# A float32 product in three parts becomes two: one of 512 columns, one of 256, and an add behind them

## Chip, cores and metric

The kernel runs on one NeuronCore of a Trainium2 chip, as one program. The time is device microseconds of one execution. The profile is one further execution under the hardware profiler, with its own time.

## The reference, cut to what matters

One sequence of 256 tokens (plus 16 meta tokens, 272 columns in all), width 1024, goes through two blocks in float32:

```python
h = h + mixer(rmsnorm(h))            # block 1: two kinds of attention, gates, w_up_a, w_up_b, w_o
h = h + hier_moe(rmsnorm(h))         #          router, then 32 experts of width 512
x = rmsnorm(h)[:, 16:]               # 256 tokens
h = h + retention_mixer(rmsnorm(h))  # block 2: 272 columns again, with its own meta tokens
h = h + swiglu(rmsnorm(h))           #          272 columns, hidden width 2816
h = h + mla_mixer(...)               #          keys over 272 columns, queries over 256
h = h + swiglu(rmsnorm(h))           #          256 columns
out = rmsnorm_2(h)[:, 16:]
```

Each `@` with a weight matrix is a dense projection; those are the subject here.

## The kernel before

Activations lie transposed: 128 features on the partitions, tokens along the free axis. `NM` = 16, `NX` = 256, `T` = 272. A dense projection works in tiles of 128 output features by `n` tokens, `n` being `T` or `NX`; each sums over `nkb` blocks of 128 input features (8 in most, 4 for `w_up_a`/`w_up_b` and the latent keys, 6 for the latent queries, 16 in the retention output, 22 in the feed-forward's second half).

Float32 is computed from two parts of the type float32r. A weight `w` is split as it arrives: ScalarE copies it to `wh` (L285), VectorE takes the rest, `wl = w - wh` (L286). The input is split in the same way into `xh`, `xl` (L285/L286, or L289/L290 with a gain). `tiles` then runs three products per weight block into one PSUM tile: `wh` by `xh` (L298), `wl` by `xh` (L299), `wh` by `xl` (L300), each of `n` columns and each with its own weight load (PEld in the profile). The tile is up to 272 columns of a PSUM bank of 512 float32; three such tiles are named `acc`, five `att`.

`dense` runs one output tile and, half way through, lets waiting generators take one step (`step`): attention, norms and transposes are written as generators that put their instructions between the projections. `begin` starts a stage with four tiles at once, first over `cut` blocks and then over the rest, so that it can start before the whole input is there; `dense` later hands those four out from `ready`. `project` adds an output to the residual `h` in two rounds, `cut` blocks first (L331), the others after the attention has ended (L336). What reads a finished tile is one VectorE or ScalarE instruction straight from PSUM: a multiply by the norm's row (L741 for the gates `sg`, L1208 and L1211 in the feed-forward, L1363 in the latent layer), `rope`'s copy (L423), the gated sums L755 and L756 in the loop over `pa` and `pb`, the residual L781 after `w_o`.

Weights come as a stream (`Stream`): fetched by DMA on SyncE's queue, split into one of five buffers of four blocks in the first block (`wsp1`), of three buffers of eight blocks in the second (`wsp2`). The expert weights (`raw<-in_wm`, 192 transfers of 1 MB) have 16 buffers, part of which lie in memory that the first block frees only when it ends.

The order of instructions on each engine is not the program's: the tile framework orders them by priority and by its own estimates of their durations when the kernel is built, and then sets the semaphores. On the chip each engine works through its list in that order.

Stages in time, by the profile: first block to about 229 us (projections, stick and sparse attention to 174, `pa`/`pb` to 198, `w_o` to 222, then the router), experts to about 710, retention, feed-forward over 272 columns, latent attention from about 1150 to 1296, feed-forward over 256 columns to 1484, final norm.

Of the kernel before, what the change touches and what calls it, by code (L numbers as in the profile page):

```python
# [16 lines left out]
P = 128  # L17
NM = 16
# [240 lines left out]
class Kern:  # L259
# [42 lines left out]
    def dense(self, ws, nkb, xh, xl, c0=0, n=T):  # L302

        if self.ready:
            return self.ready.pop(0)
        p = self.acc()
        self.tiles(ws, p, range(nkb // 2), nkb, xh, xl, c0, n)
        self.step()
        self.tiles(ws, p, range(nkb // 2, nkb), nkb, xh, xl, c0, n)
        return p[:, :n]  # L310

    def begin(self, ws, nkb, cut, xh, xl, cols, then=None, at=()):
# [3 lines left out]
        for i in range(8):  # L316
            p, (c0, n) = ps[i % 4], cols[i % 4]
            self.tiles(ws, p, range(cut) if i < 4 else range(cut, nkb), nkb, xh, xl, c0, n)
            if i in at:
                next(then, None)  # L320
        self.ready = [p[:, :n] for p, (_, n) in zip(ps, cols)]

    def project(self, ws, nkb, cut, xh, xl, c0, done):

        h, n = self.h, T - c0
        for b in range(KB):
            p = self.acc()
            self.tiles(ws, p, range(cut // 2), cut, xh, xl, 0, n)
            self.step()
            self.tiles(ws, p, range(cut // 2, cut), cut, xh, xl, 0, n)  # L330
            self.nc.vector.tensor_add(h[:, b, c0:], h[:, b, c0:], p[:, :n])  # L331
        self.flush()
        for b in range(KB):
            p = self.acc()
            self.tiles(ws, p, range(cut, nkb), nkb, xh, xl, 0, n, cut)
            self.nc.vector.tensor_add(h[:, b, c0:], h[:, b, c0:], p[:, :n])  # L336
# [125 lines left out]
    def mixer(self):  # L462
# [5 lines left out]
        with ctx:  # L468
# [21 lines left out]
            qb = m.tile([P, 4, NX], F32, name="qb")  # L490
# [38 lines left out]
            self.begin(ws, KB, 4, uh, ul, [(0, T)] * 3 + [(NM, NX)], self.rms(r, s, T, D, 1e-6), (4, 7))  # L529
# [6 lines left out]
            self.rope(kw, self.dense(ws, KB, uh, ul), T, perm, cr, sr)  # L536
            gps.memset(ckv[:, T:], 0.0)
            dve.tensor_mul(ckv[:, :T], self.dense(ws, KB, uh, ul), r)
            self.rope(ki, self.dense(ws, KB, uh, ul), T, perm, cr, sr)
# [32 lines left out]
            for b in range(4):  # L572
                self.rope(qi[:, b], self.dense(ws, KB, uh, ul, NM, NX), NX, perm, crx, srx)
# [33 lines left out]
            for b in range(4):  # L607
                if b < RAW:
                    self.expert_fetch()
                dve.tensor_mul(ka[b][:, :T], self.dense(ws, KB, uh, ul), r)  # L610
# [3 lines left out]
            for b in range(4):  # L614
                dve.tensor_mul(vt[:, b, :T], self.dense(ws, KB, uh, ul), r)
# [10 lines left out]
            for b in range(4):  # L626
                p = self.dense(ws, KB, uh, ul, NM, NX)
# [104 lines left out]
            self.gens.append(stick())  # L732
            for b in range(4):
                self.rope(qb[:, b], self.dense(ws, KB, uh, ul, NM, NX), NX, perm, crx, srx)
# [5 lines left out]
            for b in range(16):  # L740
                dve.tensor_mul(sg[b], self.dense(ws, KB, uh, ul, NM, NX), rx)  # L741
# [8 lines left out]
            for b in range(8):  # L750
                pa = self.dense(ws, 4, yah, yal, 0, NX)
                pb = self.dense(ws, 4, ybh, ybl, 0, NX)
# [25 lines left out]
            self.begin(ws, KB, 7, zh, zl, [(0, NX)] * 4)  # L778
            for b in range(8):
                p = self.dense(ws, KB, zh, zl, 0, NX)  # L780
# [12 lines left out]
            self.tiles(ws, pr, range(4), KB, hgh, hgl, 0, NX)  # L793
            rt = self.norm_end(self.colsum([s], NX), NX, D, 1e-6)
            self.tiles(ws, pr, range(4, KB), KB, hgh, hgl, 0, NX)
            lt = wk.tile([P, NX], F32, name="rp_raw")[:36]
            act(lt, pr[:36, :NX], AF.Copy)
# [396 lines left out]
    def ffn(self, u, s, c0, parts, c1, out=None):  # L1194
# [3 lines left out]
        uh, ul = u[:, 0], u[:, 1]  # L1198
# [307 lines left out]
```

## Time and profile before

| what | value |
| --- | --- |
| three runs | 1498.06, 1502.76, 1506.22 us; median 1502.76 |
| the profiled execution | 1498.93 us, span 1497.1 us |
| busy: TensorE, its weight loads, VectorE, ScalarE, GpSimd | 88%, 70%, 48%, 35%, 9% |
| granted TensorE clock, mean over the span | 0.931 of 2.4 GHz |
| DMA: moved, mean rate | 359.55 MB, 240 GB/s |

Busy shares are of the whole span. PE is TensorE's products, PEld its weight loads, which overlap them, DVE is VectorE, ACT ScalarE, POOL GpSimd, SP SyncE. A product's duration runs from its start to the modelled end of its result, so consecutive products overlap; how fast they go is read from the distance of their starts.

### The profile page before, as it was taken

To read this page: it belongs to the slowest core of one execution; us is meant where nothing else is said; L and a number is where in the kernel's file an instruction comes from. 1 tells how busy PE (TensorE), PEld (TensorE's weight loads), DVE (VectorE), ACT (ScalarE), POOL (GpSimd) and SP (SyncE) were. 2 spreads that over 40 slices of the span, in tenths; PEclk is the share of its full clock that TensorE was granted. 3 is DMA by queue.
4 is the path that set the end of the run, shared out by engine and by line. 5 is a ranking of instruction groups with operands and counts; after the bars stand their busy time and mean duration, and the time that the engine had idled before them with its cause. 6 is when DMAs were issued, how large, how long until landed. Compare 5 with 4: busy or idle time off the path is not lost.

```text
span 1497.1 us, 23804 instructions
## 1 busy us (share of the span) xinstructions
PE 1314.9 (88%) x9734; PEld 1051.7 (70%) x9734; DVE 724.4 (48%) x1417; ACT 528.3 (35%) x903; POOL 134.3 (9%) x165
## 2 busy tenths in 40 slices
PE   7999998776776666666999999999999999999997
PEld 7898993220221212104999999999999999899997
DVE  7866673110100101004666665766666865766654
ACT  5476651000000000004333443544444544544442
POOL 4010020000000000002121111100000211100001
PEclk9999998895787878778999999999999999999998
DMA  8443668999999999997434344454455433355551
GB/s 309 128 130 111 225 241 361 420 419 373 420 420 421 421 420 421 421 420 319 142 116 146 134 141 145 151 183 169 169 174 185 164 113 135 123 192 171 193 186 73
DMA packets 55266, 359.55 MB, mean 240 GB/s; under 512 B 6384, under 2 KB 7024, under 8 KB 15600
## 3 DMA queue, kind: packets, MB, share of 16 engines
q1 hardware_dynamic: 55152, 357.97, 63.2%
q8 instruction: 78, 1.28, 0.3%
q14 instruction: 36, 0.29, 0.1%
HBM read 356.90 MB, written 1.05 MB: 239 GB/s over the span
## 4 chain that ended last, share of the span: by engine, by line
PE 47%; DVE 2%; ACT 1%; issue 0%; POOL 0%; DVEq 0%; ACTq 0%; POOLq 0%
PE acc L298 14%; PE acc L300 14%; PE acc L299 14%; DVE wl L286 1%; ACT wh L285 1%; PE att L414 0%; PE att L1487 0%; PE att L1304 0%; PE att L1280 0%; PE att L383 0%; DVE U L290 0%; PE att L1306 0%; PE att L1397 0%; PE att L1294 0%; PE att L1305 0%
## 5 line engine op out<-in xcount | busy, mean ns | idle before, releaser
L298 PE MATMUL acc<-U,wh 128*128 128x272 f32 (+1 forms) x1456 | 424.0, 291 | 12.3 <-ACT U L289 7.2
L299 PE MATMUL acc<-U,wl 128*128 128x272 f32 (+1 forms) x1456 | 417.7, 287 | 2.5 <-DVE wl L286 2.5
L300 PE MATMUL acc<-U,wh 128*128 128x272 f32 (+1 forms) x1456 | 417.9, 287 | 0.0
L286 DVE TENSOR_TENSOR wl<-raw,wh 128x1024 fp32r<-128x1024 f32 x232 | 285.2, 1230 | 154.7 <-ACT wh L285 154.2
L285 ACT ACTIVATE wh<-raw 128x1024 fp32r<-128x1024 f32 x232 | 245.6, 1060 | 314.3 <-PE acc L300 211.2
L298 PEld LDWEIGHTS acc<-U,wh 128*128 128x128 f32 x1456 | 276.6, 190 | 17.6 <-ACT U L289 7.4
L299 PEld LDWEIGHTS acc<-U,wl 128*128 128x128 f32 x1456 | 275.9, 189 | 3.1 <-DVE wl L286 3.0
L300 PEld LDWEIGHTS acc<-U,wh 128*128 128x128 f32 x1456 | 275.9, 190 | 0.4
L983 PE MATMUL acc<-raw,U 128*32 128x512 f32 x1024 | 186.2, 820 | 91.0 <-DMA raw<-in_wm 87.3
L983 PEld LDWEIGHTS acc<-raw,U 128*32 128x32 f32 x1024 | 24.5, 124 | 238.1 <-DMA raw<-in_wm 214.7
L994 DVE TENSOR_TENSOR hid<-hid,acc 128x512 f32<-128x512 f32 x8 | 5.5, 688 | 258.1 <-PE acc L983 258.1
L300 PE MATMUL acc<-hl,wh 128*128 128x272 f32 (+1 forms) x352 | 99.5, 283 | 0.0
L299 PE MATMUL acc<-hh,wl 128*128 128x272 f32 (+1 forms) x352 | 99.3, 282 | 0.0
L298 PE MATMUL acc<-hh,wh 128*128 128x272 f32 (+1 forms) x352 | 99.1, 281 | 0.0
L1009 PE MATMUL att<-raw,ht 128*32 128x512 f32 x512 | 68.6, 635 | 28.7 <-DMA raw<-in_wm 25.1
L286 DVE TENSOR_TENSOR wl<-rawh,wh 128x512 fp32r<-128x512 f32 x112 | 80.5, 734 | 25.3 <-ACT wh L285 25.2
L285 ACT ACTIVATE wh<-rawh 128x512 fp32r<-128x512 f32 x112 | 68.2, 627 | 41.0 <-PE acc L300 24.9
L1018 DVE TENSOR_TENSOR h<-h,att 128x512 f32<-128x512 f32 x32 | 22.0, 688 | 123.9 <-PE att L1016 123.9
L298 PEld LDWEIGHTS acc<-hh,wh 128*128 128x128 f32 x352 | 66.4, 188 | 0.0
L300 PEld LDWEIGHTS acc<-hl,wh 128*128 128x128 f32 x352 | 66.1, 188 | 0.0
L299 PEld LDWEIGHTS acc<-hh,wl 128*128 128x128 f32 x352 | 66.1, 188 | 0.0
L373 POOL TENSOR_TENSOR s<-s,sq 128x256 f32<-128x256 f32 (+1 forms) x24 | 20.9, 886 | 493.3 <-ACT sq L369 492.8
(381 smaller groups left out, 1883.2 us busy)
## 6 DMA issues: line engine op xcount, KB each, us to landing
raw<-in_wm SPq DMA_DIRECT2D x192, 1024.0 KB, 19.9
raw<-in_ws SPq DMA_DIRECT2D x116, 1024.0 KB, 4.9
rawh<-in_ws SPq DMA_DIRECT2D x56, 512.0 KB, 3.9
const<-in_const SPq DMA_DIRECT2D x1, 1056.0 KB, 9.1
out<-Q SPq DMA_DIRECT2D x4, 256.0 KB, 2.5
h<-in_xt SPq DMA_DIRECT2D x2, 272.0 KB, 4.6
h<-in_xt SPq DMA_DIRECT2D x1, 544.0 KB, 6.6
small<-in_small SPq DMA_DIRECT2D x1, 512.0 KB, 6.2
```

The source lines that it names most:

```text
L285: self.nc.scalar.activation(hi, src, AF.Copy)
L286: self.nc.vector.tensor_sub(lo, src, hi.bitcast(F32))
L298: mm(p[:, :n], wh, xh[:, kb, c0:c0 + n], start=kb == first, stop=False)
L299: mm(p[:, :n], wl, xh[:, kb, c0:c0 + n], start=False, stop=False)
L300: mm(p[:, :n], wh, xl[:, kb, c0:c0 + n], start=False, stop=kb == nkb - 1)
L373: self.nc.gpsimd.tensor_add(s[0], s[0], t)
L983: mm(p[32 * e:32 * e + 32], XG[:, j % 2, kb, c:c + 32], w[:, 512 * e:512 * e + 512], start=kb == 0, stop=kb == KB - 1)
L994: dve.tensor_mul(hid, hid, hh[1])
L1009: mm(p[32 * e:32 * e + 32], ht[:, f * P + e * 32:f * P + e * 32 + 32], w[:, 512 * e:512 * e + 512], start=f == 0, stop=f == 3)
L1018: dve.tensor_add(h[:, k:k + 2, NM:], h[:, k:k + 2, NM:], p.rearrange("p (j n) -> p j n", j=2))
```

## The change

`tiles` takes the input as one array `x` whose second axis holds the two parts. Where `2n <= 512`, so for `n = 256` alone, a weight block makes two products: `wh` by both parts side by side, 512 columns, into both halves of the PSUM tile, and `wl` by the first part, 256 columns, into the first half. In the first block of a sum the wide product comes first, in all others the narrow one. The tile then holds two halves that have to be added: `whole` copies the second half to SBUF on ScalarE and adds the first half on VectorE, and what read PSUM before now reads that SBUF tile (two buffers). For `n = 272` the three products stay and `whole` returns the PSUM tile as it is.

```diff
-    def tiles(self, ws, p, ks, nkb, xh, xl, c0, n, first=0):
+    def tiles(self, ws, p, ks, nkb, x, c0, n, first=0):
...
         for kb in ks:
             wh, wl = ws.next()
-            mm(p[:, :n], wh, xh[:, kb, c0:c0 + n], start=kb == first, stop=False)
-            mm(p[:, :n], wl, xh[:, kb, c0:c0 + n], start=False, stop=False)
-            mm(p[:, :n], wh, xl[:, kb, c0:c0 + n], start=False, stop=kb == nkb - 1)
+            a, z = kb == first, kb == nkb - 1
+            if 2 * n <= 512:
+                both = p[:, :2 * n].rearrange("p (a n) -> p a n", a=2)
+                if a:
+                    mm(both, wh, x[:, :, kb, c0:c0 + n], start=True, stop=False)
+                mm(p[:, :n], wl, x[:, 0, kb, c0:c0 + n], start=False, stop=False, skip_group_check=True)
+                if not a:
+                    mm(both, wh, x[:, :, kb, c0:c0 + n], start=False, stop=z)
+            else:
+                mm(p[:, :n], wh, x[:, 0, kb, c0:c0 + n], start=a, stop=False)
+                mm(p[:, :n], wl, x[:, 0, kb, c0:c0 + n], start=False, stop=False)
+                mm(p[:, :n], wh, x[:, 1, kb, c0:c0 + n], start=False, stop=z)
+
+    def whole(self, p, n):
+
+        if 2 * n > 512:
+            return p[:, :n]
+        t = self.wk.tile([P, n], F32, name="whole", bufs=2)
+        self.nc.scalar.activation(t, p[:, n:2 * n], AF.Copy)
+        self.nc.vector.tensor_add(t, t, p[:, :n])
+        return t
...
         if self.ready:
-            return self.ready.pop(0)
+            return self.whole(*self.ready.pop(0))
         p = self.acc()
...
-        return p[:, :n]
+        return self.whole(p, n)
...
-            self.nc.vector.tensor_add(h[:, b, c0:], h[:, b, c0:], p[:, :n])
+            self.nc.vector.tensor_add(h[:, b, c0:], h[:, b, c0:], self.whole(p, n))
```

`project` has that last edit in both rounds. The router's tile is added in place: `act(lt, pr[:36, NX:], AF.Copy)`, then `dve.tensor_add(lt, lt, pr[:36, :NX])`. So that both parts of an input lie in one array, `hh`/`hl` become `hid`, `yh`/`yl` become `ys`, `ckh`/`ckl` and `cqh`/`cql` become `ck` and `cq`; `U`, `Q`, `yas`, `B2` and `A` were such arrays already. The tile `qb` (the sparse attention's queries) is no longer allocated at the start; it takes the buffer of `qi` (the index queries) when `qi` is no longer read.

## Rows read from the trace of the kernel before

**Rows 1.** The page: the span, and each engine's busy time.

```profile
span 1497.1 us, 23804 instructions
PE 1314.9 (88%) x9734; PEld 1051.7 (70%) x9734; DVE 724.4 (48%) x1417; ACT 528.3 (35%) x903; POOL 134.3 (9%) x165
```

**Rows 2.** Windows: stretch, its length, busy us (instructions) per engine, clock, DMA.

```profile
68.00:175.00 107.00, 106.67 (x892) 97.62 (x891) 71.21 (x170) 69.96 (x149) 6.94 (x8) 1.00 0.43 134
...
300.00:400.00 100.00, 68.50 (x392) 20.42 (x384) 10.79 (x24) 5.81 (x11) 0.00 (x0) 0.77 0.98 402
...
1200.00:1280.00 80.00, 79.97 (x622) 75.16 (x622) 46.93 (x103) 38.61 (x77) 8.63 (x13) 1.00 0.36 121
...
1300.00:1400.00 100.00, 99.95 (x833) 99.77 (x833) 64.85 (x100) 48.89 (x71) 0.00 (x0) 1.00 0.52 179
```

**Rows 3.** Windows of shorter stretches, columns PE, PEld, DVE, ACT, POOL, clock, DMA.

```profile
174.00:198.00 24.00, 23.31 (x197) 22.95 (x196) 17.77 (x37) 11.87 (x22) 5.81 (x7) 1.00 0.92 327
...
208.60:222.60 14.00, 14.00 (x124) 14.00 (x123) 13.07 (x25) 9.72 (x23) 4.19 (x6) 1.00 0.54 198
...
225.00:230.00 5.00, 2.95 (x28) 2.56 (x26) 4.26 (x24) 1.53 (x4) 0.00 (x0) 0.93 0.17 26
...
1287.50:1298.90 11.40, 8.33 (x67) 7.73 (x65) 10.95 (x18) 8.37 (x19) 5.01 (x6) 1.00 0.50 178
```

**Rows 4.** Groups by form, TensorE: names, shape, count | busy us, mean ns | idle before.

```profile
L298 PE MATMUL acc<-U,wh 128*128 128x256 f32 x616 | 175.7, 285 | 0.1
...
L298 PE MATMUL acc<-A,wh 128*128 128x256 f32 x8 | 2.3, 292 | 0.0
```

**Rows 5.** Timeline of TensorE: start us, duration us, instruction; three unbroken runs.

```profile
1000.03 0.28 PE L298 MATMUL acc<-U,wh 128*128 128x272 f32 x1
...
1002.28 0.29 PE L298 MATMUL acc<-U,wh 128*128 128x272 f32 x1
...
1350.00 0.28 PE L298 MATMUL acc<-U,wh 128*128 128x256 f32 x1
...
1352.16 0.28 PE L298 MATMUL acc<-U,wh 128*128 128x256 f32 x1
...
1439.82 0.28 PE L298 MATMUL acc<-hh,wh 128*128 128x256 f32 x1
...
1442.20 0.28 PE L298 MATMUL acc<-hh,wh 128*128 128x256 f32 x1
```

**Rows 6.** One line's products (min/median/max ns), and two groups by form.

```profile
L669 PE MATMUL att<-sb_sp,ntri x16: 352/458/542, 87.6 to 124.9; 128*128 128x416 f32 x16
...
L1487 PE MATMUL att<-sm_t,vb 128*128 128x256 f32 x16 | 4.8, 378 | 0.0
L1487 PE MATMUL att<-sm_t,vb 128*128 128x192 f32 x16 | 3.9, 326 | 0.0
```

**Rows 7.** Groups by form, ScalarE and VectorE, operations nearest to those added.

```profile
L423 ACT ACTIVATE rp_raw<-acc 128x256 f32<-128x256 f32 x11 | 4.2, 382 | 7.3 <-PE acc L300 7.3
...
L336 DVE TENSOR_TENSOR h<-h,acc 128x256 f32<-128x256 f32 x8 | 3.0, 415 | 0.3 <-PE acc L300 0.3
```

**Rows 8.** Timelines of VectorE and ScalarE in the loop over `pa` and `pb`.

```profile
192.40 0.41 DVE L755 SCALAR_TENSOR_TENSOR rp_t<-A,acc 128x256 f32<-128x256 f32 x1
...
193.33 0.41 DVE L756 SCALAR_TENSOR_TENSOR rp_u<-A,acc 128x256 f32<-128x256 f32 x1
...
194.98 0.42 ACT L285 ACTIVATE U<-rp_t 128x256 fp32r<-128x256 f32 x1 [1.91 <-POOL rp_t L757]
...
195.77 0.41 DVE L755 SCALAR_TENSOR_TENSOR rp_t<-A,acc 128x256 f32<-128x256 f32 x1
```

**Rows 9.** Timeline of TensorE at the end of `project`; in brackets the idle time.

```profile
1295.09 0.39 PE L298 MATMUL acc<-yh,wh 128*128 128x256 f32 x1 [2.66 <-DVE h L336]
```

**Rows 10.** Timelines: the first product of `project`, the last write to its input.

```profile
1263.23 0.28 PE L298 MATMUL acc<-yh,wh 128*128 128x256 f32 x1
...
1284.03 0.42 DVE L286 TENSOR_TENSOR yl<-att,yh 128x256 fp32r<-128x256 f32 x1 [1.78 <-ACT yh L285]
```

More of the change, by code (lines that the diff above doesn't have):

```diff
@@ L317, in begin, with project @@
             p, (c0, n) = ps[i % 4], cols[i % 4]
-            self.tiles(ws, p, range(cut) if i < 4 else range(cut, nkb), nkb, xh, xl, c0, n)
+            self.tiles(ws, p, range(cut) if i < 4 else range(cut, nkb), nkb, x, c0, n)
             if i in at:
                 next(then, None)
-        self.ready = [p[:, :n] for p, (_, n) in zip(ps, cols)]
-    def project(self, ws, nkb, cut, xh, xl, c0, done):
+        self.ready = [(p, n) for p, (_, n) in zip(ps, cols)]
+    def project(self, ws, nkb, cut, x, c0, done):
         h, n = self.h, T - c0
@@ L327, in project @@
             p = self.acc()
-            self.tiles(ws, p, range(cut // 2), cut, xh, xl, 0, n)
+            self.tiles(ws, p, range(cut // 2), cut, x, 0, n)
             self.step()
-            self.tiles(ws, p, range(cut // 2, cut), cut, xh, xl, 0, n)
-            self.nc.vector.tensor_add(h[:, b, c0:], h[:, b, c0:], p[:, :n])
+            self.tiles(ws, p, range(cut // 2, cut), cut, x, 0, n)
+            self.nc.vector.tensor_add(h[:, b, c0:], h[:, b, c0:], self.whole(p, n))
         self.flush()
@@ L334, in project @@
             p = self.acc()
-            self.tiles(ws, p, range(cut, nkb), nkb, xh, xl, 0, n, cut)
-            self.nc.vector.tensor_add(h[:, b, c0:], h[:, b, c0:], p[:, :n])
+            self.tiles(ws, p, range(cut, nkb), nkb, x, 0, n, cut)
+            self.nc.vector.tensor_add(h[:, b, c0:], h[:, b, c0:], self.whole(p, n))
             done(b)
@@ L792, in mixer @@
             self.flush()
-            self.tiles(ws, pr, range(4), KB, hgh, hgl, 0, NX)
+            self.tiles(ws, pr, range(4), KB, hgs, 0, NX)
             rt = self.norm_end(self.colsum([s], NX), NX, D, 1e-6)
-            self.tiles(ws, pr, range(4, KB), KB, hgh, hgl, 0, NX)
+            self.tiles(ws, pr, range(4, KB), KB, hgs, 0, NX)
             lt = wk.tile([P, NX], F32, name="rp_raw")[:36]
-            act(lt, pr[:36, :NX], AF.Copy)
+            act(lt, pr[:36, NX:], AF.Copy)
+            dve.tensor_add(lt, lt, pr[:36, :NX])
             lg = mid.tile([P, 2, 4], F32, name="lg")
@@ L1209, in ffn @@
                 act(t, t, AF.Silu)
-                p3 = self.dense(ws, KB, uh, ul, 0, n)
+                p3 = self.dense(ws, KB, u, 0, n)
                 dve.tensor_mul(t, t, p3)
-                self.split(hh[:, f], hl[:, f], t)
+                self.split(hid[:, 0, f], hid[:, 1, f], t)
             if parts:
@@ L1218, in ffn @@
             for b in range(KB):
-                p = self.dense(ws, nb, hh, hl, 0, n)
+                p = self.dense(ws, nb, hid, 0, n)
                 t = wk.tile([P, n], F32, name="ff_t")
@@ L1245, in retention @@
             dve.tensor_mul(sr, self.c("s2"), r)
[L1246 to L1247 removed]
+            ys = m.tile([P, 2, 16, T], F32R, name="ys")
             gn = self.c("g_gn")
@@ L1315, in attention @@
                     gps.tensor_mul(t[:, b], t[:, b], rs)
-                    self.split(yh[:, c], yl[:, c], t[:, b])
+                    self.split(ys[:, 0, c], ys[:, 1, c], t[:, b])
             for hd in range(4):
@@ L1330, in retention @@
             done, s = self.prep([(u, "g_ffn0", 0)], 0)
-            self.project(ws, 16, 12, yh, yl, 0, done)
+            self.project(ws, 16, 12, ys, 0, done)
             return u, s
@@ L1351, in latent, with latent_in @@
             kr = m.tile([P, T], F32, name="kr")
-            self.rope(kr, self.dense(ws, KB, kh, kl), T, perm, cr, sr)
-            def latent_in(name, nb, xh, xl, n, gain, rr, skip, after=None):
-                ch = m.tile([P, nb, n], F32R, name=name + "h")
-                cl = m.tile([P, nb, n], F32R, name=name + "l")
+            self.rope(kr, self.dense(ws, KB, u), T, perm, cr, sr)
+            def latent_in(name, nb, x, n, gain, rr, skip, after=None):
+                cs = m.tile([P, 2, nb, n], F32R, name=name)
                 rn = m.tile([P, n], F32, name=name + "r")
@@ L1375, in after @@
                 dve.tensor_mul(srq, self.c("s3")[:, NM:], rq)
-            cqh, cql, rq = latent_in("cq", 6, qh, ql, NX, "g_qa", r[:, NM:], 1, after)
-            yh = m.tile([P, 8, NX], F32R, name="yh")
-            yl = m.tile([P, 8, NX], F32R, name="yl")
+            cq, rq = latent_in("cq", 6, qq, NX, "g_qa", r[:, NM:], 1, after)
+            ys = m.tile([P, 2, 8, NX], F32R, name="ys")
             with self.tc.tile_pool(name="mlah", bufs=2, reuse_waits="tile") as w:
@@ L1438, in latent @@
                 done, s = self.prep([(u, "g_ffn1", NM)], NM)
-                self.project(ws, 8, 6, yh, yl, NM, done)
+                self.project(ws, 8, 6, ys, NM, done)
             return u, s
```

80 lines of the change are left out of this document (37 added, 43 removed).

## Prediction, made before the change was run

> **What bounds the kernel now.** I read the page first, for the span and the shares. The span is 1497.1 us and its run took 1498.93 us; TensorE is busy for 88% of the span, VectorE for 48%, ScalarE for 35% [rows 1]. These shares are averages over stages with different limits, so the second view is busy time by stage [rows 2]. There the reader is to see three kinds. In the first block's projections (68 to 175 us), in the latent attention (1200 to 1280) and in the last feed-forward (1300 to 1400) TensorE has no gap, and VectorE fills 59 to 67% of the time. In the expert stage the DMA engines are full (0.98) and TensorE works 68.5 us of 100. A smaller cut of the same view finds the stages where VectorE is the engine without room [rows 3]: 13.07 of 14.0 us while the output projection `w_o` ends, 10.95 of 11.4 us at the end of the latent layer's `project`, where TensorE idles for 3 us. Just after the first block's last products the DMA share is 0.17: the expert weights wait for that block's memory. So whatever moves the end of the first block moves the full-DMA stretch behind it and everything after that by as much.
>
> **How many products change.** Only calls with 256 columns change. The nine groups of L298 at 256 columns, the first and the last of which stand in [rows 4], count 616, 176, 72, 64, 48, 32, 32, 24 and 8: 1072 triples. Each triple (weights' first part by the input's first part, second by first, first by second: 3 x 256 columns, three weight loads) becomes one product of 512 columns and one of 256, with two loads. The columns stay 768; one product and one load in three go. The 272-column products do not change.
>
> **What a product costs.** Steps from start to start in an unbroken run [rows 5]: 18 products in 1352.16 - 1350.00 = 2.16 us, so 120.0 ns at 256 columns; 18 in 2.25 us, 125.0 ns, at 272; in the last feed-forward's second half 21 in 2.38 us, 113.3 ns. The granted clock is 1.00 there [rows 2], the 2.4 GHz level, at which 256 columns are 106.7 ns: 13.3 ns (6.7 in the second half) go to something else. No row has a 512-column product of this type (float32r) with fresh weights, so I bound it. Nearest is L669, same type, 416 columns: its shortest is 352 ns against 285 for 256 columns [rows 4, 6], 67 ns for 160 columns, hence 107 ns for 256 more and a step of 120 + 107 = 227. The float32 products of L1487 pass twice; 64 more columns (128 passes) cost 378 - 326 = 52 ns [rows 6], so 104 for 256 passes and a step of 224. The bounds: 213.3 ns (512 columns at the clock, nothing besides) and 240 ns (twice 120, the excess going with columns). I take 227, by the row of the same type. The triple goes from 360 to 227 + 120 = 347, a gain of 13 ns; in the second half from 340 to 113.3 + 107 + 113.3 = 333.6, a gain of 6.4.
>
> The rows and a rule differ here. The Trainium skill, page "TensorE: Matmul & The Clock Gate", section "Wait — 56ns, not 53.3ns?", gives back-to-back products as N / 2.4 GHz plus about 2.5 ns. By that rule alone the triple would lose only 2.5 ns, where the rows' 13.3 ns of excess lets it lose 13. The trace disagrees with the rule at 256 columns (120.0 ns measured, 109.2 by the rule).
>
> **Where the gain counts.** Only where TensorE is the limit. First block up to the projections' end: 28 tiles x 8 = 224 triples. Latent layer: 12 query tiles x 6 = 72 and the first part of `project`, 8 x 6 = 48. Last feed-forward, first half: 44 x 8 = 352. Together 696 x 13 ns = 9.0 us. Second half: 176 x 6.4 ns = 1.1 us. Sum 10.1 us. The other 200 triples (`pa`/`pb` and `w_o` 128, router 8, latent `cq` 48, second part of `project` 16) sit where VectorE or a chain sets the pace, or come out even, and I count nothing for them.
>
> **What `whole` adds.** Each of 138 tiles gets a ScalarE copy of its second half out of PSUM and a VectorE add of the first half, ahead of the operation that read the tile before. Nearest rows [rows 7]: 382 ns for a ScalarE copy of this shape from PSUM, 415 ns for a VectorE add with one operand there. That is 52.7 us of ScalarE and 57.3 us of VectorE, plus 0.8 us of latency per tile. Behind a waiting copy on ScalarE stand the next weight splits; the products they feed have three buffers of weights (in the first block five, of half the size), so a split has about two tiles of 8 x 360 ns = 2.9 us to come. So in the stages of [rows 2] I cost it at nothing: from 68 to 175 us VectorE goes from 71.2 to about 71.2 + 24 x 0.42 = 81 of 105 us, in the last feed-forward from 65 to about 65 + 35 x 0.42 = 80 of 96, and TensorE's weights still come first. If that cover were gone, each tile would show up to 0.8 us. For `cq` I set its 48 x 13 ns = 0.6 us against the delay of its six tiles and count nothing.
>
> Where the cover is missing:
> - `pa`/`pb` (174 to 198 us). VectorE goes round a loop: the add of gate times product (L756), GpSimd's sum, ScalarE's split (L285 at 194.98), VectorE's rest, the next L755; from 192.40 to 195.77 that is 3.37 us per output block [rows 8], against 2.8 of products. Two more adds in it, about 0.33 us apart, make 4.03, over eight blocks +5.3 us; at the other end they fit in VectorE's waits for ScalarE, +0. I take +4, nearer the loop, because the adds sit ahead of L755 and L756.
> - `w_o` and the router: 13.07 of 14.0 us are taken [rows 3], eight adds x 0.415 = 3.3 us; bounds 1 (the free 0.9 and the shorter products) and 4. I take +3, and +0.4 for the router's add on its chain.
> - End of `project`: 10.95 of 11.4 us taken, TensorE waits 2.66 us for L336 to give a PSUM tile back [rows 9]. Eight more adds: +3.3, eight copies on ScalarE besides (8.37 of 11.4 used, 3.1 more): +3, bounds 2 and 4.5.
> - The last tile of the program: +0.8, copy and add.
> Sum +11.2 us.
>
> The moved `qb`, now in `qi`'s buffer, waits for the index scores' last product, long done when `qb` is written; the joined tiles (`hid`, `ys`, `ck`, `cq`) move no work. Both cost nothing; the cover is the projections in between, and without it one tile, 2.8 us, would wait.
>
> **Sum.** 1498.93 - 10.1 + 11.2 = 1500.0 us against the profiled execution's own time. That run lies 3.83 us under the median of the three (1502.76), so the same +1.1 us against the median is 1503.9: I say 1504. Half a per cent, 7.5 us, is about what a measurement of this kernel can tell from no change.
>
> **Rivals.**
> A, faster: the 512-column product has no excess at all (213.3 ns). Then the triple gains 26.7 ns, 696 of them 18.6 us, the second half 13.3 x 176 = 2.3; -20.9 + 11.2 = -9.7, 1493 us. For: two-pass float32 rows, whose slope lies near the bare clock. Against: L669's own slope. It decides below 216 ns. Chance 0.20.
> B, slower: the excess belongs to columns, not to products; the 512-column product takes 240 ns. No gain is left, +11.2, 1514 us. For: 113.3 and 120.0 ns for the same shape show that the excess is no constant of a product. Against: 272 columns cost 5 ns more than 256, not 5% of 120 more. It decides above 236 ns. Chance 0.14. The rule of the Trainium skill's page "TensorE: Matmul & The Clock Gate" named above would end on this side too, with 2.5 ns a triple.
> C, slower: copy and add both stand in the loop of `pa`/`pb` in full, two tiles x 0.8 us per block: eight blocks x 1.6 = 12.8 us in place of 4. That is +9.9, 1513 us. For: ScalarE is in that loop too, and works in order. Against: it was busy only 11.87 of 24 us [rows 3]. It decides from 4.7 us per block. Chance 0.15.
> D, slower: a product that reads both parts at once waits for the whole stretch between them. The first product of `project` starts at 1263.23 while the last part of its input is written from 1284.03 [rows 10]: up to 21 us lost, 1525 us. Nothing in the trace speaks for it, as no product there reads two places. Chance 0.06.
>
> The forecast, gain and loss nearly equal, has 0.45; its own range is 1497 to 1511. Faster by over 0.5% is A, 0.20; slower B, C and D, 0.35. The range for eight in ten runs from 1490, a little under A, to 1519, over B and C; D and a gain beyond A are left out.
>
> **What would show it.** Right: L298-type products of 512 columns stepping 227 ns before a 256-column one of 120; 1300 to 1400 us shorter by 3 to 4%; the first block's end later by some 5 us, its L755 period near 4 us; TensorE's gap before the last feed-forward near 6 us in place of 3. Wrong: steps near 213 or 240 ns (A, B); a `pa`/`pb` period near 5 us (C); the first product of `project` after 1284 us (D); or gaps of TensorE in the stages that I call covered, with ScalarE's copies ahead of the weight splits.

## The result, and the profile after

The changed kernel took 1511.14 us (median of six runs, 1510.22 to 1512.3); the kernel before, run beside it, 1503.1. The ratio of the mean times is 1.0059, 95% interval 1.0043 to 1.0075: 8.9 us slower, where 1.1 were forecast. One of the six runs before, at 1559.45 us, was a slow one, which counts in the median 1503.1 but not in the ratio; the two medians differ by 8.0 us. The time lies in the range of 1490 to 1519, just past the end of the likeliest case's own (1511); it is slower by just over the half per cent that the prediction called the limit of a measurement. The profiled execution took 1510.22 us.

The page of the changed kernel, against [rows 1]:

```profile
span 1508.4 us, 21864 instructions
...
PE 1321.9 (88%) x8662; PEld 1002.0 (66%) x8662; DVE 776.6 (51%) x1556; ACT 573.2 (38%) x1041; POOL 134.0 (9%) x165
```

1072 products and as many loads are gone. VectorE does 52.2 us more and ScalarE 44.9. TensorE's busy time did not fall.

The groups by form of the changed kernel: the wide and the narrow product on the input `U`, then the new copy and add (last column: idle time ahead of them).

```profile
L307 PE MATMUL acc<-U,wh 128*128 128x512 f32 x539 | 196.2, 398 | 0.1
L305 PE MATMUL acc<-U,wl 128*128 128x256 f32 x616 | 163.3, 286 | 1.1 <-DVE wl L286 1.0
...
L319 DVE TENSOR_TENSOR whole<-whole,acc 128x256 f32<-128x256 f32 x135 | 56.1, 419 | 40.3 <-ACT whole L318 39.1
L318 ACT ACTIVATE whole<-acc 128x256 f32<-128x256 f32 x135 | 51.0, 382 | 76.2 <-PE acc L307 73.0 <-DVE rp_t L775 1.5 <-DVE wl L286 1.4
```

Copy and add cost what [rows 7] had (382 and 415 ns): 382 and 419.

TensorE's timeline of the changed kernel (start us, duration us), in the last feed-forward's first half and, in the last two lines, in its second:

```profile
1360.72 0.39 PE L307 MATMUL acc<-U,wh 128*128 128x512 f32 x1
1360.96 0.28 PE L305 MATMUL acc<-U,wl 128*128 128x256 f32 x1
1361.07 0.39 PE L307 MATMUL acc<-U,wh 128*128 128x512 f32 x1
...
1362.12 0.39 PE L307 MATMUL acc<-U,wh 128*128 128x512 f32 x1
...
1450.17 0.39 PE L307 MATMUL acc<-hid,wh 128*128 128x512 f32 x1
...
1451.92 0.39 PE L307 MATMUL acc<-hid,wh 128*128 128x512 f32 x1
```

Four triples take 1.40 us in the first half, five take 1.75 in the second: 350 ns both times. Over 1312 to 1420 us the mean step from a wide product to the narrow one behind it is 233.1 ns (264 of them), from a narrow one to the next wide one 119.2. In the first half that is a gain on 360 [rows 5]; in the second it is a loss against 3 x 113.3 = 340.

Windows of the changed kernel (columns as in [rows 2, 3]), the first three over the same stretches as [rows 2], the rest over those of [rows 3], moved along with the stages:

```profile
68.00:175.00 107.00, 107.00 (x702) 87.51 (x702) 79.52 (x198) 76.69 (x172) 6.90 (x8) 1.00 0.45 143
300.00:400.00 100.00, 66.42 (x376) 17.81 (x368) 8.20 (x15) 5.22 (x10) 0.00 (x0) 0.78 0.97 400
1200.00:1280.00 80.00, 78.89 (x522) 69.06 (x522) 53.74 (x124) 40.12 (x82) 10.04 (x15) 1.00 0.36 120
...
174.80:200.80 26.00, 23.96 (x130) 19.16 (x129) 21.90 (x51) 15.72 (x37) 5.91 (x7) 1.00 0.85 287
216.50:230.50 14.00, 13.92 (x80) 12.03 (x79) 12.38 (x25) 9.34 (x24) 3.92 (x5) 0.88 0.32 110
...
1298.50:1309.90 11.40, 7.12 (x36) 5.58 (x37) 10.37 (x24) 8.13 (x21) 4.12 (x5) 1.00 0.36 138
```

Read the two stretches of the first block first. From 174.8 to 200.8 VectorE is busy 21.90 of 26 us where it was 17.77 of 24, and TensorE has 2 us without a product. At the end of `w_o` VectorE is nearly as full as before (12.38 us, 13.07 then), but the granted clock is 0.88 in place of 1.00, and DMA is down at 0.32. The timeline of TensorE shows what happened there:

```profile
215.58 0.49 PE L304 MATMUL acc<-U,wh 128*128 128x512 f32 x1 [1.82 <-DVE whole L319]
...
217.44 0.41 PE L305 MATMUL acc<-U,wl 128*128 128x256 f32 x1
...
218.08 0.41 PE L305 MATMUL acc<-U,wl 128*128 128x256 f32 x1
```

By the profile TensorE waits 1.82 us for a PSUM tile that the new add holds, and a little later a triple takes 640 ns in place of 350 (217.44 to 218.08): the lower clock level, from 216.6 us for 3.4 us. Five triples take 3.20 us there, 1.45 more than at 350 ns. TensorE's waits for VectorE from 174 to 231 us (total us, times, longest), first before and then after:

```profile
PE acc L298 <- DVE rp_t L755: 0.7, 2, 0.4
```

```profile
PE acc L305 <- DVE wl L286: 2.4, 4, 0.8
PE acc L304 <- DVE whole L319: 1.8, 1, 1.8
```

So 4.2 of the 4.5 us that TensorE waits there after the change are waits for VectorE: for the rest of a weight's split (L286) and for the add of a tile (L319). VectorE's timeline in the loop over `pa` and `pb`, against [rows 8]:

```profile
191.63 0.42 DVE L775 SCALAR_TENSOR_TENSOR rp_t<-A,whole 128x256 f32<-128x256 f32 x1
194.44 0.42 DVE L775 SCALAR_TENSOR_TENSOR rp_t<-A,whole 128x256 f32<-128x256 f32 x1
199.37 0.42 DVE L775 SCALAR_TENSOR_TENSOR rp_t<-A,whole 128x256 f32<-128x256 f32 x1
203.78 0.42 DVE L775 SCALAR_TENSOR_TENSOR rp_t<-A,whole 128x256 f32<-128x256 f32 x1
```

The period is 2.8 to 3.1 us at first and 4.9 and 4.4 for the last two blocks; seven periods take 178.25 to 203.78, 3.65 us each, where 4.03 was worked out; before, the same seven took 3.33 us each (175.83 to 199.14). At the end of `project`, against [rows 9], TensorE's timeline has three waits of together 4.69 us (2.66 before):

```profile
1298.98 0.50 PE L304 MATMUL acc<-ys,wh 128*128 128x512 f32 x1 [0.90 <-DVE whole L319]
...
1301.93 0.50 PE L304 MATMUL acc<-ys,wh 128*128 128x512 f32 x1 [1.27 <-DVE whole L319]
...
1306.13 0.50 PE L304 MATMUL acc<-ys,wh 128*128 128x512 f32 x1 [2.52 <-DVE whole L319]
```

And against [rows 10], timelines of TensorE and VectorE:

```profile
1272.33 0.39 PE L304 MATMUL acc<-ys,wh 128*128 128x512 f32 x1
...
1293.20 0.42 DVE L286 TENSOR_TENSOR ys<-att,ys 128x256 fp32r<-128x256 f32 x1 [1.11 <-ACT ys L285]
```

The first product of `project` still starts 21 us ahead of the last write to its input: a product that reads both parts did not wait here for what lies between them.

**Where the time went.** Stages from the first product of each to the first of the next (the router and the second half to the end of their last product), in us, from TensorE's timeline, for before, after, and three experiments told below (three products everywhere; these and the add alone; wide products without the add):

| stage | before | after | three products | add alone | wide alone |
| --- | --- | --- | --- | --- | --- |
| to the first product of `pa` | 174.13 | 174.84 | 174.63 | 176.97 | 174.18 |
| `pa`/`pb` and `w_o` | 48.11 | 55.28 | 49.36 | 53.92 | 48.50 |
| router | 3.92 | 5.37 | 3.92 | 4.78 | 3.99 |
| experts | 469.60 | 472.76 | 471.83 | 471.92 | 470.47 |
| retention to latent keys | 473.28 | 469.26 | 466.72 | 469.13 | 475.77 |
| latent queries and heads | 94.19 | 94.82 | 94.19 | 97.27 | 94.07 |
| `project` | 32.68 | 34.60 | 32.67 | 34.79 | 32.67 |
| last feed-forward, first half | 128.60 | 125.94 | 128.60 | 129.64 | 126.20 |
| second half | 60.01 | 61.94 | 62.34 | 60.01 | 61.94 |
| rest | 12.61 | 13.64 | 12.16 | 13.47 | 12.76 |
| span | 1497.13 | 1508.45 | 1496.42 | 1511.90 | 1500.55 |

The experts and the stretch from retention to the latent keys have no product of 256 columns, and yet they vary by 3 and 9 us between kernels. In the second of them this goes with the granted clock: in that stretch it was at the lower level for 4.6 us in the shortest (three products, 466.72), 13.7 before and 20.5 in the longest (wide alone, 475.77). The edits change no product and add no operation in these stages, what lowers the clock in one kernel and not in another is open, and the stages that the change touches are read by themselves. In those the change costs 12.2 us, 9.3 up to the router and 2.9 behind it.

### The profile page after: what moved, and what is told of

Read it like the earlier page. It is cut to its first block, busy times and chain, and to the rows that moved or that the text cites. A ratio compares the mean times of both kernels' runs of the same rounds, so it can differ in the third digit from the quotient of the medians.

```text
span 1508.4 us, 21864 instructions
## 1 busy us (share of the span) xinstructions
PE 1321.9 (88%) x8662; PEld 1002.0 (66%) x8662; DVE 776.6 (51%) x1556; ACT 573.2 (38%) x1041; POOL 134.0 (9%) x165
## 3 DMA queue, kind: packets, MB, share of 16 engines
HBM read 356.90 MB, written 1.05 MB: 237 GB/s over the span
## 4 chain that ended last, share of the span: by engine, by line
PE 47%; DVE 3%; ACT 1%; issue 0%; POOL 0%; DVEq 0%; ACTq 0%; POOLq 0%
PE acc L309 9%; PE acc L311 9%; PE acc L307 9%; PE acc L310 9%; PE acc L305 5%; DVE wl L286 1%; PE acc L304 1%; ACT wh L285 1%; PE att L434 1%; PE att L403 1%; PE att L1501 0%; PE att L1321 0%; PE att L1297 0%; PE att L1323 0%; DVE U L290 0%
## 5 line engine op out<-in xcount | busy, mean ns | idle before, releaser
L286 DVE TENSOR_TENSOR wl<-raw,wh 128x1024 fp32r<-128x1024 f32 x232 | 285.4, 1231 | 121.4 <-ACT wh L285 118.2
L309 PE MATMUL acc<-U,wh 128*128 128x272 f32 x840 | 248.7, 296 | 10.2 <-ACT U L289 7.3
L310 PE MATMUL acc<-U,wl 128*128 128x272 f32 x840 | 244.5, 291 | 2.4 <-DVE wl L286 2.4
L311 PE MATMUL acc<-U,wh 128*128 128x272 f32 x840 | 245.1, 292 | 0.0
L307 PE MATMUL acc<-U,wh 128*128 128x512 f32 x539 | 196.2, 398 | 0.1
L309 PEld LDWEIGHTS acc<-U,wh 128*128 128x128 f32 x840 | 160.4, 191 | 13.5 <-ACT U L289 7.5
L305 PE MATMUL acc<-U,wl 128*128 128x256 f32 x616 | 163.3, 286 | 1.1 <-DVE wl L286 1.0
L311 PEld LDWEIGHTS acc<-U,wh 128*128 128x128 f32 x840 | 160.7, 191 | 0.4
L307 PEld LDWEIGHTS acc<-U,wh 128*128 128x128 f32 x539 | 102.1, 189 | 20.0 <-DVE U L286 0.3
L286 DVE TENSOR_TENSOR wl<-rawh,wh 128x512 fp32r<-128x512 f32 x112 | 81.4, 743 | 13.9 <-ACT wh L285 13.2
L318 ACT ACTIVATE whole<-acc 128x256 f32<-128x256 f32 x135 | 51.0, 382 | 76.2 <-PE acc L307 73.0
L319 DVE TENSOR_TENSOR whole<-whole,acc 128x256 f32<-128x256 f32 x135 | 56.1, 419 | 40.3 <-ACT whole L318 39.1
```

The lines of the kernel that those rows point to most:

```text
L286: self.nc.vector.tensor_sub(lo, src, hi.bitcast(F32))
L305: mm(p[:, :n], wl, x[:, 0, kb, c0:c0 + n], start=False, stop=False, skip_group_check=True)
L307: mm(both, wh, x[:, :, kb, c0:c0 + n], start=False, stop=z)
L309: mm(p[:, :n], wh, x[:, 0, kb, c0:c0 + n], start=a, stop=False)
L310: mm(p[:, :n], wl, x[:, 0, kb, c0:c0 + n], start=False, stop=False)
L311: mm(p[:, :n], wh, x[:, 1, kb, c0:c0 + n], start=False, stop=z)
```

## The experiments

**Which block.** A switch in `tiles` and `whole` turns single stages back to three products (arrays stay joined). First the first block, then everything behind it:

```diff
-            if 2 * n <= 512:
+            if 2 * n <= 512 and self.wide:
...
-        if 2 * n > 512:
+        if 2 * n > 512 or not self.wide:
```

> The first block has the three products of before, without copy and add; the latent layer and the last feed-forward stay as changed. Theory 1 (the loss is the copy and the add at the end of the first block, where VectorE and ScalarE had no room: w_o, router, pa/pb, about 9 us, and the expert stage moves with it): ratio to before 1.000 to 1.002, some 10 us under the changed kernel. Theory 2 (the loss is the wide product, which steps 232 ns in place of 227, and is spread over all stages): half of the 1072 triples lie in the second block, so ratio 1.003 to 1.005. Both: the up half of the last feed-forward 3 us shorter than before, its down half 2 us longer.

> The reverse: the first block as changed, the latent layer and the last feed-forward with the three products of before. Theory 1: the whole loss of the first block is there, ratio 1.006 to 1.008, the first block's last products end about 9 us later than before. Theory 2: ratio 1.002 to 1.004. If the two halves add up, the excesses over before of this run and of the one with the first block undone sum to that of the changed kernel, 0.0059.

Measured: 1502.04 us, ratio 1.0001 (0.9984 to 1.0018), with the first block undone; 1511.56 us, 1.0069 (1.0045 to 1.0093), with the second undone. That is theory 1: the cost comes from the first block. That the second block neither wins nor loses is not shown, though: by the table its stages lose 2.9 us in the changed kernel, 0.19%, just outside the first run's interval.

**Which half of the edit.** The add alone: three products of 256 columns, the third into the second half of the PSUM tile, then `whole`. And the wide products alone, without copy and add (this leaves the products of `wh` and the input's second part out of the sum, except in the router).

```diff
...
-                    mm(both, wh, x[:, :, kb, c0:c0 + n], start=False, stop=z)
...
+                mm(p[:, :n], wh, x[:, 0, kb, c0:c0 + n], start=a, stop=False)
...
+                mm(p[:, n:2 * n], wh, x[:, 1, kb, c0:c0 + n], start=False, stop=z, skip_group_check=True)
```

> Three products of 256 columns as before, but the third goes into the second half of the PSUM tile, and copy and add stand behind every tile as in the changed kernel. Theory 1: all of the loss and none of the gain, ratio 1.008 to 1.011; the last feed-forward's two halves take their times of before (128.8 and 60.0 us) within 1 us. Theory 2: copy and add are hidden, ratio 0.999 to 1.002.

> Wide products as in the changed kernel, but no copy and no add: readers take the first half of the tile alone, so the product of the weights' first part with the input's second is left out of the result (the router keeps its add). Theory 1: the products alone gain 352 x 8.8 ns = 3.1 us in the up half of the last feed-forward and about 2 us in the first block's and latent projections, and lose 176 x 11 ns = 2 us in the down half: ratio 0.996 to 0.999. Theory 2: the loss stays, ratio 1.004 to 1.007.

Measured: the add alone 1514.65 us, ratio 1.0098 (1.0068 to 1.0127), 14.7 us slower; the wide products alone 1498.7 us, 0.9981 (0.9966 to 0.9997), 2.9 us faster. Timelines of TensorE, the first product of `pa` with the add alone and with the wide products alone:

```profile
176.97 0.28 PE L302 MATMUL acc<-yas,wh 128*128 128x256 f32 x1
```

```profile
174.18 0.40 PE L304 MATMUL acc<-yas,wh 128*128 128x512 f32 x1
```

By the table the add alone costs 2.3 us in the first block's projections against three products without it, 3.1 in the latent queries and heads, 1.0 in the last feed-forward's first half. These are stages where I had called it covered. Not all of it is the add's own, though. First a wait of TensorE in the latent stage with the add alone, then the same wait in the kernel before; behind them, with the add alone, the last wait in `project` and a window at the start of the feed-forward:

```profile
1191.13 1.00 PE L431 MATMUL att<-const,rs_z 128*128 128x128 f32 x6 [1.59 <-DVE rs_z L377]
```

```profile
1180.71 1.00 PE L414 MATMUL att<-const,rs_z 128*128 128x128 f32 x6 [0.70 <-DVE rs_z L360]
```

```profile
1307.98 0.39 PE L302 MATMUL acc<-ys,wh 128*128 128x256 f32 x1 [2.51 <-DVE whole L316]
```

```profile
1308.90:1312.30 3.40, 3.40 (x18) 3.40 (x17) 2.94 (x8) 3.40 (x9) 1.54 (x2) 0.50 0.36 147
```

In both stages the granted clock is at its lower level for 3.4 us, from 1192.8 and from 1308.9 us, and products of 256 columns step 213 ns in place of 120, some 1.5 us lost each time. So the feed-forward's 1.0 us is the clock, and copy and add are covered there. Of the latent stage's 3.1 us 1.5 are the clock and 0.9 a longer wait for VectorE, which works there at the root of a norm (`rs_z`). In the first block's projections the clock stays at 1.00.

The wide products alone gain 2.4 us in the feed-forward's first half and at most 0.5 us in the two others, where the attention's own products stand between the tiles. From 26 us to the first product of `pa` the steps out of dense products come to 1.9 us less than before (102.83 us in place of 104.69; 224 x 7.7 ns would be 1.7), and the steps out of all other products to 1.8 us more (45.15 in place of 43.39). Why those became longer is not shown: the profile has a single TensorE wait there, of 0.2 us. With copy and add in place the wide products do gain in these stages too, 2.1 us in the projections and 2.5 in the latent stage (after against the add alone, 1.5 of the latter the clock). By the table the changed stages of the wide products alone come to +0.1 us, as the second half gives back 1.9; the 2.9 us of the runs, uncertain by 2.3, are not found in any stage.

**The end of the first block.** Only `pa`/`pb`, `w_o` and the router back to three products:

```diff
+            self.wide = False
             for b in range(8):
                 pa = self.dense(ws, 4, yas, 0, NX)
...
```

> Only `pa`/`pb`, `w_o` and the router go back to three products read as before; the first block's projections and everything behind the first block stay as changed. Theory 1 (the loss is made by copy and add in these three places): the router's first product starts at 224.5 to 225.5 us (changed kernel 230.12, before 222.24), the run lies near 1503 to 1505 us, ratio 1.000 to 1.002. Theory 2 (the copies and adds of the projections before them already made VectorE late, and the tail only shows it): the router's first product still starts after 228 us, and the run stays near 1510 us.

Only `w_o` as changed in the first block, and only `pa`/`pb`:

> The first block as before but for `w_o`, which is as changed; everything behind the first block as changed. Between the first product of `w_o` and that of the router lie 24.42 us before, 29.36 after, 24.56 with the whole first block undone. Theory 1a (the eight adds and the last tile's copy are `w_o`'s own cost, 3.3 + 0.8): 28 to 29.5 us. Theory 2a (`w_o` pays for being entered late from `pa`/`pb`, with a late VectorE and late weights): 24.5 to 26.5 us, and then `pa`/`pb` is the dear part. Run by 1a about 1508 us, by 2a about 1505.

> The counterpart of the run with `w_o` alone as changed: in the first block only `pa`/`pb` has the wide products with copy and add, everything behind the first block is as changed. From the first product of `pa` to the router's lie 48.11 us before, 50.08 with the whole first block in three products, 51.08 with `w_o` alone changed, 55.28 with all changed. Theory 4 (the sixteen adds of `pa`/`pb` are the dear part, since VectorE leaves that stage behind and has no room in `w_o` to catch up): 53 to 54.5 us here, `w_o` itself, whose code is that of before, 27 us or more, the run 1507 to 1509 us. Rival (neither part is dear alone, and only both together fill VectorE): 51 to 52 us, `w_o` 25 to 26, the run 1504 to 1506 us.

Measured: 1506.75 us, ratio 1.0028 (1.0018 to 1.0039), with the end undone; 1507.15 us, 1.0029 (1.0016 to 1.0042), with `w_o` alone; 1503.84 us, 1.0020 (1.0008 to 1.0031), with `pa`/`pb` alone. The first products of `pa` and of the router on TensorE's timeline, first with `w_o` alone and then with `pa`/`pb` alone:

```profile
174.59 0.28 PE L309 MATMUL acc<-yas,wh 128*128 128x256 f32 x1
...
225.67 0.28 PE L309 MATMUL acc<-A,wh 128*128 128x256 f32 x1
```

```profile
173.94 0.39 PE L304 MATMUL acc<-yas,wh 128*128 128x512 f32 x1
...
224.50 0.28 PE L309 MATMUL acc<-A,wh 128*128 128x256 f32 x1
```

That is 51.08 and 50.56 us where three products take 49.36 and everything changed 55.28. Theory 4 falls, and the rival's figures come out or nearly (`w_o` 25.14 us; both stages 50.56, named 51 to 52; run 1503.84, named 1504 to 1506): `pa`/`pb` is not the dear part. `w_o` alone, 26.49 us, is at the upper end of theory 2a and below 1a, but its run of 1507.15 us is nearer to 1a's 1508 than to 2a's 1505. With the end undone the two took 51.71 us: some of the loss may come with the projections in front, and theory 1 of that run (router from 224.5 us, 1503 to 1505) is 1 to 2 us short. There is no single dear part. By the ratios, over the run with the whole first block undone, the projections cost 4.1 us (1.0028 less 1.0001), `w_o` 4.2 and `pa`/`pb` 2.9, together 11 where all of the first block costs 8.7; each of these is uncertain by some 3 us. The profiles are little sharper: the same code for the whole first block took 55.28 us here in the changed kernel and 53.46 with the second block undone, three products 48.1 to 50.3 in four kernels. Most of the first difference is the lower clock. The windows of `w_o` with the second block undone and in the changed kernel:

```profile
201.26:228.44 27.18, 24.88 (x146) 21.02 (x144) 23.20 (x45) 17.18 (x40) 5.76 (x7) 1.00 0.59 195
```

```profile
200.76:230.12 29.36, 26.62 (x146) 22.24 (x144) 23.21 (x45) 17.22 (x40) 5.67 (x7) 0.94 0.53 179
```

Without the 1.45 us of the clock `w_o` takes 27 to 28 us as changed, about 3 more than with three products.

**VectorE's operation or ScalarE's copy.** `w_o` without `whole`; VectorE adds both halves straight out of PSUM:

```diff
...
-                dve.scalar_tensor_tensor(h[:, b, NM:], p, 0.5, h[:, b, NM:], op0=ALU.mult, op1=ALU.add)
+                for i in (0, 1):
+                    dve.scalar_tensor_tensor(h[:, b, NM:], p[:, i * NX:i * NX + NX], 0.5, h[:, b, NM:], op0=ALU.mult, op1=ALU.add)
```

> As changed, but in `w_o` no `whole`: two VectorE additions take the two halves straight out of PSUM into the residual, each about 0.42 us, so that VectorE has as much to do and ScalarE has no copy. Theory 1a (VectorE's extra operation is the price): from the first product of `w_o` to the router's 28.5 to 29.5 us, as with the changed kernel (29.36). Theory 2b (the ScalarE copy is, as it stands ahead of the weight splits and makes VectorE wait): 25.5 to 27 us, and the run is 3 us shorter than the changed one.

Measured: `w_o` to the router 28.53 us (29.36 as changed), run 1510.04 us, ratio 1.0043 (1.0023 to 1.0062). It is at the lower end of theory 1a, and theory 2b falls for the stage. TensorE's two longest waits from 174 to 231 us are again for VectorE: 2.4 us in all for weights' rests (L286) and 2.0 for the add straight from PSUM (L808). So VectorE's extra operation is the price as far as the waits show it. What the copy adds is not shown: without the lower clock, which this run did not have in `w_o`, the version with the copy takes 27 to 28 us, no more than this one; and by the ratios the run is 2.4 us under the changed kernel, near 2b's 3, with intervals that overlap.

**The queue of transfers.** The edit does not touch a DMA, but SyncE's queue is in another order. Its timeline before and after, loads of expert weights (the loads of `in_ws` between them are left out):

```profile
193.82 0.43 SPq L1036 DMA_DIRECT2D raw<-in_wm  x1
...
203.92 0.43 SPq L1036 DMA_DIRECT2D raw<-in_wm  x1
...
212.52 0.42 SPq L1036 DMA_DIRECT2D raw<-in_wm  x1
```

```profile
188.40 0.42 SPq L1057 DMA_DIRECT2D raw<-in_wm  x1
...
196.50 0.42 SPq L1057 DMA_DIRECT2D raw<-in_wm  x1
...
215.65 0.39 SPq L1057 DMA_DIRECT2D raw<-in_wm  x1
```

The first two of these, the eighth and the ninth load of 1 MB, have passed ahead of three and four loads of weights for the first block, and ScalarE's split of these waits 5.5 us for transfers from 198 to 232 us, 1.6 before. So I held six loads behind at least as many weight loads as before, in the changed kernel and in the one with the end undone:

```diff
...
+        j = {3: 41, 4: 43, 5: 45, 6: 48, 7: 50, 8: 53}.get(self.nraw)
+        if j:
+            with self.tc.issue_after(self.wloads[j - 1].ins):
+                self.nc.sync.dma_start(w, self.a["wm"][g, c])
...
```

> The changed kernel in full, but six loads of expert weights on SyncE's queue are held behind as many weight loads of the first block as in the kernel before (there the seventh to ninth stand behind 48, 50 and 53 of them, in the changed kernel behind 45, 47 and 49). Theory 1 (copy and add in `w_o` are its whole price): first product of `w_o` to that of the router stays 28.5 to 29.5 us. Theory 3 (part of the price is that the newly built order lets expert weights pass ahead of the weights that `w_o` waits for): 26 to 27.5 us, as where only `w_o` was changed (26.49), ScalarE's waits for weight transfers fall from 5.5 us to 4 or less, and the run is about 2 us shorter than the changed kernel, 1508 to 1509.

> As the run with `pa`/`pb`, `w_o` and the router in three products, with the same six loads of expert weights held back as before. There `w_o`, whose code is that of before, took 26.55 us to the router in place of 24.42. Theory 3 (the queue's order made that): 24.4 to 25.4 us here, the run 1 to 2 us shorter. Rival (VectorE comes late out of the projections in front): it stays above 26 us.

Measured in the changed kernel: 1511.38 us, ratio 1.0055 (1.0037 to 1.0072), `w_o` 29.93 us, with 3.4 us of the lower clock in it as in the changed kernel. Theory 3 falls there. The groups of ScalarE from 198 to 232 us, before, after, and with the old queue (last columns: idle time and what ended it):

```profile
L285 ACT ACTIVATE wh<-rawh 128x512 fp32r<-128x512 f32 x15 | 8.8, 621 | 2.6 <-DMA rawh<-in_ws 1.6 <-PE acc L300 0.9
```

```profile
L285 ACT ACTIVATE wh<-rawh 128x512 fp32r<-128x512 f32 x18 | 10.7, 624 | 7.0 <-DMA rawh<-in_ws 5.5 <-issue 1.5
```

```profile
L286 ACT ACTIVATE wh<-rawh 128x512 fp32r<-128x512 f32 x16 | 9.4, 621 | 4.9 <-DMA rawh<-in_ws 4.2 <-PE acc L308 0.5
```

ScalarE's wait for transfers fell by 1.3 us and the stage did not end earlier. With the end undone the old queue took `w_o` from 26.55 to 25.50 us and the run to 1505.24 us, 1.0020 (1.0008 to 1.0032). The rival (above 26 us) falls, and theory 3 nearly comes out (24.4 to 25.4, 1 to 2 us shorter). But the 1 us is about the spread of that stage between kernels with the same code there (24.42 to 25.41), and ScalarE waits longer for transfers with the old queue (4.7 us, where without it none was of note), so the queue is not shown to be the cause.

**What is left without the change, and one stage alone.** Three products everywhere with the joined arrays; and wide products in the last feed-forward's first half alone.

> Three products everywhere; left of the change are the joined arrays and `qb` in `qi`'s buffer. Theory 1 (those cost nothing): every stage within a us of before but for the clock, `pa`/`pb` 23.7 us, second half of the last feed-forward 60.0, 1500 to 1505 us. Rival (they shift the order that is built, and VectorE reaches `pa`/`pb` later): `pa`/`pb` takes 24.6 to 25.5 us, as in the four runs that had its code undone.

> Wide products only in the first half of the two feed-forwards' code, which touches the last feed-forward's 352 triples alone; everything else three products (arrays joined). Theory 1 (a triple gains 8.8 ns where TensorE has no gap and the copies are covered; joining arrays costs nothing): that half takes 126.0 us in place of 128.6, no other stage moves but by the clock; 1500 us, ratio 0.998, faster than both kernels but by less than half a per cent. Rival (joining the arrays costs something by itself): second half near 61.9 us in place of 60.0, or the first block longer by a us or more; ratio 1.000 or above.

Measured: 1498.19 us in one run for the first; `pa`/`pb` takes 24.65 us, so the rival is half right: about 1 us of what looks like the price of `pa`/`pb` (23.69 before) is there without any wide product. The second: 1499.34 us, ratio 0.9978 (0.9963 to 0.9994), the lowest ratio measured. Its first half on TensorE's timeline runs from the first to the second of these starts, 125.91 us:

```profile
1300.24 0.63 PE L304 MATMUL acc<-U,wh 128*128 128x512 f32 x1
...
1426.15 0.28 PE L309 MATMUL acc<-hid,wh 128*128 128x256 f32 x1
```

Both of these kernels have a second half of 62.34 us with three products. Its step there, from the timeline with joined arrays alone (21 products in 2.47 us), is 117.6 ns:

```profile
1439.94 0.28 PE L309 MATMUL acc<-hid,wh 128*128 128x256 f32 x1
...
1442.41 0.28 PE L309 MATMUL acc<-hid,wh 128*128 128x256 f32 x1
```

The kernel before had 113.3 [rows 5], as had the two experiments with 60.01 us, which have joined arrays too. So joining alone is not the reason. The rival of the second run has its two stage figures (second half 62.34 us, the first block's end 1.9 us later than before) and not its ratio. That the wide products are what makes this version 3.3 us faster than before is not shown by the run times: joined arrays alone ran once, and that run was shorter still (1498.19 us). What the trace shows of them is the first half, 2.7 us shorter.

## Why the prediction was right, and what was off

Gain and loss of some ten microseconds each, nearly equal, was the forecast. The measured parts are smaller on one side and larger on the other: wide products alone -2.9 us (forecast -10.1), copy and add alone +14.7 (forecast +11.2; in its profiled execution two spells of the lower clock make some 3 us), and both together +8.9, as each hides some of the other. The size of the gain is the term that was off most.

The range held by its width. A kernel slower by over half a per cent was given to rivals B, C and D, with a chance of 0.35 in sum, and none of the three happened: the time moved to their side because most of the gain stayed out. B had named that, but by a product of 240 ns, not by stages that do not get shorter. Of the signs of being right, the step (233 ns), the period (3.65 us, named 4) and TensorE's gap before the last feed-forward (4.69 us, named 6) came near; the feed-forward's first half got 2.1% shorter, where 3 to 4% were named, and the first block's end came 9.3 us later, not 5.

- **The 512-column product, 227 ns:** 233.1. Rival A (below 216) falls and so does B (above 236). The triple gains 360 - 352.3 = 7.7 ns, not 13; over 352 triples that is 2.7 us, and the stage got 2.66 shorter. That 227 came so near is in part luck: it set L669's shortest product, 352 ns, against a mean of 285. The shortest of L298 with 256 columns is 276 ns; shortest against shortest gives 76 ns for 160 columns and a step of 242, on rival B's side. By the Trainium skill, page "TensorE: Matmul & The Clock Gate", section "Wait — 56ns, not 53.3ns?", back-to-back products step N / 2.4 GHz plus about 2.5 ns, an estimate of 215.8 ns for 512 columns; the trace disagrees by 17 ns at 512 columns as it does by 10 at 256.
- **The gain on 696 triples:** this is the step that failed. It reached the end of the stage only in the last feed-forward's 352. In the first block's projections 2.9 us were forecast and 0.7 lost, no more than kernels with three products there differ (173.85 to 174.63); in the latent queries and heads 0.9 forecast, 0.6 lost. A TensorE without gaps was read as a TensorE whose dense products set the pace. In the projections these did get 1.9 us shorter, and the other products in TensorE's list took 1.8 us longer; what held those up is not shown.
- **The second half, -1.1 us:** +1.9. 340 ns became 352 (61.94 us over 176). But the 113.3 ns that it was taken from is one of two rates that the same shape shows there; against the other (117.6) the change gains 0.4 us.
- **Copy and add at nothing in the full stages:** right in the feed-forward's first half, where the 1.0 us of the add alone is the clock; wrong where attention runs along, 2.3 us in the projections and 1.6 in the latent stage without its spell of the lower clock. The attention's chain behind the same two engines was not looked at.
- **`pa`/`pb` +4 and `w_o` +3:** together +7.2 (+5.3 with the second block undone), where 7 was forecast; split otherwise, 2.2 and 4.9, of which 1.45 us is the lower clock, which no term had, and about 1 us was there with three products. So the 7 came out by luck; what is left of it, 4 to 5 us, goes with TensorE's waits for VectorE. The period rose by 0.32 us, half of the 0.66 that was put in for two adds. C falls: 3.65 us a period, and it needed 4.7 (only the last two, 4.9 and 4.4, were near).
- **Router +0.4:** +1.45. **End of `project` +3, less 0.6 of its gain:** +1.9. **Last tile +0.8:** +1.0.
- **D** falls, by the start of `project` at 1272.33.

Over the profiled pair these misses, with their signs, are 3.6 (projections), 1.6 (latent), 1.9 and 3.1 (feed-forward), 1.05 (router), 0.4 (`pa`/`pb`, `w_o`, last tile) less 0.5 (`project`) and 0.9 (stages without a changed product): 10.2, from +1.1 to the +11.3 of the two spans.

Open is what selects the rate of 113 or 118 ns in the second half, what starts a spell of the lower clock, and how the first block's loss divides between its parts: their shares are no larger than the 1 to 2 us by which that stretch differs between kernels with the same code in it.

## What to carry to other kernels

Fewer, wider products save only the start of each, here 8 ns of 360, and only the stage gets shorter by it in which those products set the pace. A split sum then has to be put together again, and that costs where VectorE has no room: here 7.2 us for the 24 tiles of `pa`/`pb` and `w_o`, 0.3 us each, the clock included, and nothing in the feed-forward's first half. Put such an edit into the one stage where its products set the pace and the engines behind them have room, and leave it out elsewhere. Before a difference between two kernels is put down to an edit, look at the granted clock of that stage in both. When an instruction is added, compare the order of all queues too, since the builder may move transfers that the edit does not name, and then test whether that order mattered before blaming it.

## What of the hardware was unexpected

A product's excess over its columns at 2.4 GHz was 13.3 ns at 256 columns and 19.8 at 512 (233.1 - 213.3): neither one constant per product nor in proportion to the columns. The same 256-column products ran a whole stage at 113.3 ns a step in three kernels and at 117.6 in two, at a granted clock of 1.00 each time. And a TensorE gap of 1.82 us at the end of `w_o` was followed by the lower clock level, 640 ns a triple in place of 350, for 3.4 us. A gap does not do that each time: of two nearly equal ones at the end of `project`, 2.51 us with the add alone was followed by 3.4 us at the lower level, and 2.52 us in the changed kernel by none.
